# Entrance and gathers of a 32-expert mixture rebuilt: norm split without its shift, gathers of four experts, routing first, 16 weight buffers

## The chip, the core and the metric

The kernel runs on one core of a Trainium2 chip. The metric is device time in microseconds (us) from launch to end. Three runs of the kernel before took 2071.98 to 2072.4 us, median 2072.03.

## The reference, cut to what matters

256 tokens of width 1024, fp32, go through two hybrid blocks (state space and dilated attention, with gated feed-forward layers) and then through a second block: a convolution and gated-linear-attention mixer, a mixture of 32 experts, and a final modulated norm. The change touches the end of that mixer, the mixture and the final norm:

```python
h = h + ga1[:, None, :] * y                       # y = merged @ w_out (mixer)
u2 = modulate(rmsnorm(h, g_norm2[l]), sh2, sc2)   # norm * (1 + sc2) + sh2
y2 = hierarchical_moe(u2, ...)
h = h + ga2[:, None, :] * y2
return modulate(rmsnorm(h, g_final), shf, scf)

def hierarchical_moe(h, w_rg, b_rg, w_re, b_re, w1, w3, w2):
    lg = (t @ w_rg + b_rg); gsel = top_k(lg, 1)          # one of 4 groups
    le_sel = (t @ w_re + b_re) of that group             # its 8 experts
    top_v, top_i = lax.top_k(le_sel, 2)                  # two of them
    ...
    for e in range(32):
        hid = jax.nn.silu(t @ w1[e]) * (t @ w3[e])       # 1024 -> 512
        y = y + comb[:, e:e + 1] * (hid @ w2[e])         # 512 -> 1024
```

The weights of the 32 experts are 192 MB in fp32, and each of them has to come from HBM once.

## The kernel before, in words

The engines run from queues in program order; a scheduler of tiles puts in the semaphores. The words below go stage by stage through the end of the program.

**End of the mixer** (`mixer2`, lines 955 to 992). The product with `w_out` is made in two halves of 512 columns. After each half, VectorE makes the residual stream `x` of both 128-token tiles and `xg = x * G2`, where `G2` is the gain of the second norm times (1 + scale); TensorE transposes `xg` and multiplies it with the router's weights (L980); ScalarE takes the squares for the norm. `rsqrt` (L71 to L87) makes the reciprocal root in 12 small VectorE operations, after which L989 writes the 36 logits of each tile.

**Norm of the experts' input** (`norm2`, L1329). VectorE makes u = xg * rstd + sh2 for each tile (L1335), ScalarE its rounded part `u2h` (L1340), GpSimd the rest `u2l` (L1341). The pair hi + lo lets TensorE copy rows exactly.

**Routing** (`route`, L1197). Some 20 small VectorE operations find group, experts and weights; a prefix sum on TensorE (L1237, L1238) gives each token its slot in its expert, `pos` (L1240). An expert has 64 slots. A second part (L1244 on) makes the weights and counts.

**Gathers** (`gather`, L1412). For a batch of `BATCH = 8` experts VectorE compares the slot numbers with `pos` and so makes a one-hot matrix `sel` [256 tokens, 8 x 64] (L1417). For each of the 8 chunks kc of the model width, four matmuls (u2h and u2l, two token tiles) of 512 columns write the gathered inputs to a PSUM bank, and VectorE or ScalarE copy them to `T` (L1435, L1437). Batch 0 is gathered up front; each later batch is made beside the experts of the batch before it. `paced(..., 2, 1)` and `tick` drop one chunk (one piece) of a gather into TensorE's program at points between weight tiles. The pieces use the pool `tp` of two PSUM banks, which the transposes of the hidden layer and `slots` use too.

**Experts** (`experts`, L1530), in 16 pairs. A pair uses the two 64-column halves of the array, one expert each: `project` (L1469) for w1 and w3, `hidden` (transposes L1484, Silu L1488, product L1490), `down` (L1504) for the pair before, and `spread` (L1522), which adds the weighted rows into four accumulator banks. The weights come in pieces of 1 MB, 12 for a pair, on SyncE's DMA queue (L1392). There are RAWB + RAW2 + RAW3 + RAW4 = 4 + 3 + 2 + 3 = 12 buffers of 1 MB; a new load is issued when the matmuls of two buffers have been issued (`halves`, L1405).

**End** (`finish_rows` L1343, `finish` L1358). The rows of the last norm are loaded and made by GpSimd during the entrance. The tail multiplies the accumulators with ga2, adds the residual, takes the norm and writes out.

Of the kernel before, what the change touches and what calls it, by code (L numbers as in the profile page):

```python
# [9 lines left out]
F32 = mybir.dt.float32  # L10
# [38 lines left out]
class Kern:  # L49
# [21 lines left out]
    def rsqrt(self, src, n, scale, pool=None):  # L71

        nc, pool = self.nc, pool or self.small
        m = self.t(pool, [P, n], "nw_m")
        md = m.rearrange("p (a b) -> p a b", a=src.shape[1]) if len(src.shape) == 3 else m
        nc.vector.tensor_scalar(md, src, scale, EPS, op0=ALU.mult, op1=ALU.add)  # L76
        t = self.t(pool, [P, n], "nw_t")
        y = self.t(pool, [P, n], "nw_y", bufs=6)
        nc.vector.tensor_scalar(t.bitcast(I32), m.bitcast(I32), 1, None, op0=ALU.arith_shift_right)  # L79
        nc.vector.tensor_scalar(  # L80
            y.bitcast(I32), t.bitcast(I32), -1.0, float(0x5F3759DF), op0=ALU.mult, op1=ALU.add
        )
# [746 lines left out]
    def mixer2(self):  # L829
        nc, a, tc = self.nc, self.a, self.tc  # L830
        w_in = a["w_in_2"][0]
        with ExitStack() as outer:
# [124 lines left out]
            self.ss = self.t(self.small, [P, 2, 2], "ss", bufs=2)  # L957
            pl = [self.t(self.ax, [P, 512], "ax") for _ in range(2)]
            xTs = self.t(keep, [P, 2, D], "o")
            for nb in range(2):  # L960
                sl = slice(nb * 512, (nb + 1) * 512)
                ps = self.gemm_x(a["w_out_2"][0], nb * 512, 512, self.xh, self.xl)
                xT = xTs[:, nb, :].rearrange("p (c t) -> p c t", c=4)
                done = None
                for t in range(2):
                    with tc.issue_after(done) if done else ExitStack():
                        m = self.t(self.tmp, [P, 512], "xg")
                        nc.vector.tensor_mul(m, ps[t], ga1[:, sl])
# [4 lines left out]
                    for j in range(4):  # L973
                        nc.tensor.transpose(pt[:, j, :], xg[:, j * P : (j + 1) * P], self.ident)
                    nc.scalar.activation(xT[:, :, t * P : (t + 1) * P], pt, AF.Copy)
                    sq = self.t(self.tmp, [P, 512], "sq", bufs=1)
                    nc.scalar.activation(sq, self.x[:, t, sl], AF.Square, accum_out=self.ss[:, t, nb : nb + 1])
                    for j in range(4):
                        kc = nb * 4 + j
# [4 lines left out]
                if nb == 0:  # L984
                    self.moe_more()
            self.prep_end()
# [210 lines left out]
    def route(self, pool):  # L1197
# [36 lines left out]
        nc.vector.tensor_add(mb, o1, o2)  # L1234
# [3 lines left out]
        nc.tensor.matmul(pp[:, 32:64], self.ones, mb[:, 0, :], start=False, stop=True)  # L1238
        pos = self.t(pool, [P, 2, 32], "pos")
# [70 lines left out]
    def moe_final(self):  # L1310
        nc, a, tc = self.nc, self.a, self.tc
        with ExitStack() as ctx:
# [9 lines left out]
            route = self.route(lp)  # L1322
            self.norm2(lp, u2h, u2l)
            pos = next(route)
            rows = self.finish_rows(lp)
            comb, cnt = self.experts(lp, u2h, u2l, route, pos, acc)
            self.finish(lp, acc, rows, cnt, comb)

    def norm2(self, lp, u2h, u2l):  # L1329

        nc = self.nc
        w = self.t(lp, [P, 4, D], "T")
        for t in range(2):
            u = w[:, t, :]
# [8 lines left out]
    def finish_rows(self, lp):  # L1343

        nc, a = self.nc, self.a
        rows = [self.t(lp, [P, D], f"fin{j}") for j in range(3)]
        for dst, idx in zip(rows, (5, 7, 6)):
            nc.gpsimd.dma_start(dst, self.modd[0:1, idx * D : (idx + 1) * D].to_broadcast([P, D]))
        g = a["g_final_2"].rearrange("(o n) -> o n", o=1)
        for nb in range(2):  # L1350
            sl = slice(nb * 512, (nb + 1) * 512)
            gr = self.t(lp, [P, 512], "gu", bufs=4)
            nc.gpsimd.dma_start(gr, g[:, sl].to_broadcast([P, 512]))
            nc.gpsimd.tensor_scalar(rows[1][:, sl], rows[1][:, sl], 1.0, None, op0=ALU.add)
            nc.gpsimd.tensor_mul(rows[1][:, sl], rows[1][:, sl], gr)
        return rows

    def finish(self, pool, acc, rows, cnt, comb):  # L1358
        nc = self.nc
        ga2, Gf, shf = rows  # L1360
        yz = self.t(pool, [P, 4, D], "T")
        y, z = yz[:, 0:2, :], yz[:, 2:4, :]
# [49 lines left out]
    def gather(self, pool, b, u2h, u2l, pos, out, banks=None):  # L1412
# [12 lines left out]
        for kc in range(KD):  # L1425
            sl = slice(kc * P, (kc + 1) * P)
            pg = banks[kc % 4] if banks else self.t(self.tp, [P, 512], "tp")
            pg = pg.rearrange("p (e s) -> p e s", e=BATCH)
            for n, src in enumerate((u2h, u2l)):
                for t in range(2):  # L1430
                    nc.tensor.matmul(
                        pg, src[:, t, sl], sel[:, t], start=n == 0 and t == 0, stop=n == 1 and t == 1
                    )
# [96 lines left out]
    def experts(self, pool, u2h, u2l, route, pos, acc):  # L1530
# [6 lines left out]
        nxt = self.beside(self.gather(pool, 0, u2h, u2l, pos, batch, acc[0] + acc[1]))  # L1537
        sel0 = next(nxt[0])
        for e in range(0, NEXP, 2):
            b, ei = divmod(e, BATCH)  # L1540
            if ei == 0:
                self.drain(nxt)
                sel, T = batch
                if e == 0:
                    with self.tc.issue_after(sel0):
                        comb, combs, cnt = next(route)
# [4 lines left out]
            x = T[:, :, ei : ei + 2, :]  # L1551
            slots = self.beside(self.slots(pool, sel, ei, e, combs, so))
            gu = [self.project(pool, x, on_scalar)]
# [8 lines left out]
            last = h, so  # L1562
        self.drain()
        self.down(pool, NEXP - 2, last[0][0], *last[1], acc)
        self.drain()
        return comb, cnt

    def overflow(self, pool, cnt, comb, y, z, ga2):
# [3 lines left out]
        with tc.If(big > CAP):  # L1572
            w = self.t(self.s2, [P, 4, D], "T")
            G2, g, sh2, u = (w[:, j, :] for j in range(4))
            u2T = z.rearrange("p a b -> p (a b)").rearrange("p (k t) -> p k t", k=KD)
            nc.gpsimd.dma_start(G2, self.modd[0:1, 4 * D : 5 * D].to_broadcast([P, D]))
            nc.gpsimd.dma_start(g, a["g_norm2_2"].to_broadcast([P, D]))
            nc.gpsimd.dma_start(sh2, self.modd[0:1, 3 * D : 4 * D].to_broadcast([P, D]))
            nc.vector.scalar_tensor_tensor(G2, G2, 1.0, g, op0=ALU.add, op1=ALU.mult)
            for t in range(2):  # L1580
# [3 lines left out]
                nc.vector.tensor_add(u, u, sh2)  # L1584
                for k in range(KD):
                    pt = self.t(self.tp, [P, 512], "tp")
                    nc.tensor.transpose(pt[:, :P], u.rearrange("p (q k) -> p k q", k=KD)[:, k, :], self.ident)
                    nc.scalar.activation(u2T[:, k, t * P : (t + 1) * P], pt[:, :P], AF.Copy)
            nc.vector.memset(y, 0.0)
            with tc.For_i(0, NEXP, 1) as e:  # L1590
# [3 lines left out]
                hid = self.t(pool, [P, 4, 256], "gu_o")  # L1594
# [208 lines left out]
```

## Time and profile before

| | |
|---|---|
| median of 3 runs | 2072.03 us (2071.98 to 2072.4) |
| profiled execution, time | 2072.26 us |
| profiled execution, span from first to last instruction | 2070.4 us |
| mean granted TensorE clock (1 is 2.4 GHz) | 0.984 |
| TensorE busy | 1975.3 us, 95% of the span |
| VectorE, ScalarE, GpSimd busy | 60%, 43%, 10% |
| first matmul of an expert's weights begins | 1570.22 us |
| last matmul of the experts begins | 2052.42 us |

Rows of the trace give start and duration in us, engine (PE is TensorE, PEld its weight loads, DVE VectorE, ACT ScalarE, POOL GpSimd, SP SyncE), line, operation, output <- inputs, partitions x elements, and in brackets how long the engine stood idle before it, and what it waited for. A row with xN stands for N like instructions in a run. The end of a matmul is modelled, so starts are safer to subtract than durations. PEclk is the granted clock.

### The profile page before, as it was taken

The page shows a single profiled execution, that of the slowest core. Times are in us where ns is not written, and L with a number is a line of the kernel's source. Part 1 is how long each engine was busy: PE and PEld are TensorE (multiplying, and loading weights), DVE is VectorE, ACT ScalarE, POOL GpSimd, SP SyncE. Part 2 cuts the span into 40 slices and gives each one's busy share as a digit, 9 for nine tenths or more (in the row PEclk, how much of TensorE's full clock was granted, in tenths as well). Part 3 has the DMA queues.
Part 4 walks back from the last instruction along what each step waited for, and adds up shares of the span by engine and source line. Part 5 has one row for each costly group of instructions (what it writes and reads, how often), then busy time and mean ns, then how long its engine had stood idle before and what let it go on. Part 6 is the DMA issues. An engine that isn't in the chain of part 4 may idle for free. (4 is left out here: it accounts for less than half of the span.)

```text
span 2070.4 us, 25452 instructions
## 1 busy us (share of the span) xinstructions
PE 1975.3 (95%) x9734; PEld 1442.8 (70%) x9734; DVE 1232.4 (60%) x2027; ACT 899.3 (43%) x1371; POOL 217.3 (10%) x300
## 2 busy tenths in 40 slices
PE   8999999999999999999999999889978999999996
PEld 6888978788888888987788888877864433333332
DVE  5874897778766775797876556999762111110113
ACT  5444666645444444575745444766531111111111
POOL 1000222000000000023000000653011000000001
PEclk9999999999999999999999999999988999999998
DMA  8875543447776875542546556444766999999994
GB/s 276 283 276 189 163 138 102 160 162 259 262 251 225 269 253 178 181 162 82 166 135 201 182 171 205 124 132 153 266 224 253 421 418 375 421 367 421 420 420 177
DMA packets 193100, 493.11 MB, mean 238 GB/s; under 512 B 11832, under 2 KB 47600, under 8 KB 168400
## 3 DMA queue, kind: packets, MB, share of 16 engines
q1 hardware_dynamic: 185760, 479.32, 64.1%
q0 software_dynamic: 4992, 11.49, 1.9%
q8 instruction: 78, 1.28, 0.3%
q10 hardware_dynamic: 2224, 0.66, 0.2%
q14 instruction: 46, 0.38, 0.1%
HBM read 490.34 MB, written 1.08 MB: 237 GB/s over the span
## 5 line engine op out<-in xcount | busy, mean ns | idle before, releaser
L128 DVE TENSOR_TENSOR lo<-raw,hi 128x1024 fp32r<-128x1024 f32 (+1 forms) x462 | 572.8, 1240 | 290.1 <-ACT hi L127 289.7
L127 ACT ACTIVATE hi<-raw 128x1024 fp32r<-128x1024 f32 (+1 forms) x462 | 486.4, 1055 | 532.3 <-PE mm L174 462.5
L173 PE MATMUL mm<-lo,xh 128*128 128x512 f32 (+2 forms) x1200 | 460.4, 384 | 10.9 <-DVE lo L128 10.9
L172 PE MATMUL mm<-hi,xh 128*128 128x512 f32 (+2 forms) x1200 | 465.7, 389 | 0.4 <-ACT hi L127 0.4
L174 PE MATMUL mm<-hi,xl 128*128 128x512 f32 (+2 forms) x1200 | 459.3, 383 | 0.0
L173 PEld LDWEIGHTS mm<-lo,xh 128*128 128x128 f32 x1200 | 227.6, 190 | 59.4 <-DVE lo L128 15.1
L174 PEld LDWEIGHTS mm<-hi,xl 128*128 128x128 f32 x1200 | 227.4, 189 | 45.8
L172 PEld LDWEIGHTS mm<-hi,xh 128*128 128x128 f32 x1200 | 227.5, 190 | 45.6 <-ACT hi L127 0.8
L1469 PE MATMUL mm<-raw,T 128*64 128x512 f32 x1024 | 242.4, 596 | 0.0
L1469 PEld LDWEIGHTS mm<-raw,T 128*64 128x64 f32 x1024 | 72.9, 137 | 139.8 <-issue 137.1
L1504 PE MATMUL mm<-raw,H 128*64 128x512 f32 x512 | 148.6, 600 | 10.1 <-DVE gu L1474 10.1
L172 PE MATMUL mm<-hi,hh 128*128 128x512 f32 x352 | 139.1, 395 | 0.0
L174 PE MATMUL mm<-hi,hl 128*128 128x512 f32 x352 | 138.9, 394 | 0.0
L173 PE MATMUL mm<-lo,hh 128*128 128x512 f32 x352 | 138.5, 394 | 0.0
L1474 DVE COPY gu<-mm 128x512 f32<-128x512 f32 x16 | 11.1, 692 | 178.6 <-PE mm L1469 168.8
L1504 PEld LDWEIGHTS mm<-raw,H 128*64 128x64 f32 x512 | 45.9, 136 | 85.5 <-issue 62.5
L1512 ACT ACTIVATE yh<-mm,wsl 128x512 fp32r<-128x512 f32 x32 | 22.0, 688 | 181.7 <-PE mm L1504 181.7
L191 PE MATMUL mm<-xh,lo 128*128 128x256 f32 x320 | 91.2, 285 | 3.4 <-DVE lo L128 3.4
L189 PE MATMUL mm<-xh,hi 128*128 128x256 f32 x320 | 91.1, 287 | 0.8 <-ACT hi L127 0.8
L190 PE MATMUL mm<-xl,hi 128*128 128x256 f32 x320 | 91.2, 285 | 0.4 <-DVE xl L204 0.4
L759 DVE SCALAR_TENSOR_TENSOR macc<-raw,cact,macc 128x512 f32<-128x512 f32 x112 | 83.9, 749 | 2.4 <-DMA raw<-in_w_ada_dram 0.3
L1513 DVE SCALAR_TENSOR_TENSOR yl<-mm,wsl,yh 128x512 fp32r<-128x512 f32 x32 | 24.0, 750 | 94.3 <-ACT yh L1512 93.0
(428 smaller groups left out, 2739.1 us busy)
## 6 DMA issues: line engine op xcount, KB each, us to landing
raw<-in_w_dram SPq DMA_DIRECT2D x192, 1024.0 KB, 10.0
raw<-in_w_in_dram SPq DMA_DIRECT2D x71, 1024.0 KB, 5.2
raw<-in_ffn_w_up_dram SPq DMA_DIRECT2D x44, 1024.0 KB, 6.8
raw<-in_ffn_w_gate_dram SPq DMA_DIRECT2D x43, 1024.0 KB, 5.2
raw<-in_ffn_w_down_dram SPq DMA_DIRECT2D x40, 1024.0 KB, 5.1
raw<-in_w_ada_dram SPq DMA_DIRECT2D x24, 1024.0 KB, 5.3
raw<-in_w_out_dram SPq DMA_DIRECT2D x20, 1024.0 KB, 5.1
raw<-in_w_ada_f_dram SPq DMA_DIRECT2D x8, 1024.0 KB, 5.4
```

The lines of the kernel that those rows point to most:

```text
L127: nc.scalar.activation(h, r, AF.Copy)
L128: nc.vector.tensor_tensor(l, r, h.bitcast(F32), op=ALU.subtract)
L172: nc.tensor.matmul(ps[t][:, :w], xh[:, kc, sl], hi, start=kc == 0, stop=False)
L173: nc.tensor.matmul(ps[t][:, :w], xh[:, kc, sl], lo, start=False, stop=False)
L174: nc.tensor.matmul(ps[t][:, :w], xl[:, kc, sl], hi, start=False, stop=kc == kt - 1)
L189: nc.tensor.matmul(o, hi[:, sl], xh[:, kc, :], start=kc == 0, stop=False)
L190: nc.tensor.matmul(o, hi[:, sl], xl[:, kc, :], start=False, stop=False)
L191: nc.tensor.matmul(o, lo[:, sl], xh[:, kc, :], start=False, stop=kc == kt - 1)
L759: last = nc.vector.scalar_tensor_tensor(acc, raw[:, k, :], c, acc, op0=ALU.mult, op1=ALU.add)
L1469: nc.tensor.matmul(pg[s * CAP : (s + 1) * CAP, :], x[:, kc, s, :], w[:, k, :], start=kc == 0, stop=kc == KD - 1,)
L1504: nc.tensor.matmul(pd[nb][q, :], H[:, c, q], w[s][:, k, nb * 512 : (nb + 1) * 512], start=c == 0, stop=c == 3,)
L1513: nc.vector.scalar_tensor_tensor(yl, pd[nb], ws, yh.bitcast(F32), op0=ALU.mult, op1=ALU.subtract)
```

## The change

- The second half of the product with `w_out` is made in two parts of 256 columns, each with its own residual, transposes, router matmuls and squares. The three sums of squares are added by one reduction.
- `rsqrt` takes 10 operations in place of 12 (other constants, two steps in place of three).
- The split of the norm leaves out the shift: `u2h` is xg * rstd rounded by ScalarE (four instructions of 512 columns, strided), `u2l` the rest by VectorE (four, in `lows`). The shift `sh2`, now a column per chunk, is added where the gathered rows leave PSUM. GpSimd has no part in it.
- VectorE goes from the logits straight to routing; one `lows` operation stands ahead of `pos`, three behind `sel`. The second part of the routing comes after the first projection.
- A batch of the gather is four experts: 8 batches in place of 4, matmuls of 256 columns in place of 512. Batch 0 uses four accumulator banks at a time, u2h matmuls first.
- The rows of the last norm are loaded by SyncE behind the last expert weights, into weight buffers, and combined by one VectorE operation there.
- Weight buffers: 4 + 4 + 2 + 6 = 16 of 1 MB. `T` of half the size and the rows that are gone make room.

```diff
-RAW2 = 3
+RAW2 = 4
 RAW3 = 2
-RAW4 = 3
-BATCH = 8
+RAW4 = 6
+BATCH = 4
...
-            for nb in range(2):
-                sl = slice(nb * 512, (nb + 1) * 512)
-                ps = self.gemm_x(a["w_out_2"][0], nb * 512, 512, self.xh, self.xl)
+            for i, (c0, w) in enumerate(((0, 512), (512, 256), (768, 256))):
+                sl = slice(c0, c0 + w)
+                n = w // P
+                ps = self.gemm_x(a["w_out_2"][0], c0, w, self.xh, self.xl)
...
-            self.prep_end()
+            s2 = self.t(self.small, [P, 2], "ss2", bufs=2)
+            nc.vector.tensor_reduce(s2, ss, axis=AX.X, op=ALU.add)
+            self.rstd = self.rsqrt(s2, 2, 1.0 / D)
...
+        with self.tc.issue_after(done):
+            lows.pop(0)()
         pos = self.t(pool, [P, 2, 32], "pos")
...
-            nc.vector.scalar_tensor_tensor(
-                u.rearrange("p (k q) -> p q k", k=KD), self.xg[:, t, :].rearrange("p (q k) -> p q k", k=KD),
-                self.rstd[:, t : t + 1], self.sh2.rearrange("p (q k) -> p q k", k=KD),
-                op0=ALU.mult, op1=ALU.add,
-            )
-            nc.scalar.activation(u2h[:, t, :], u, AF.Copy)
-            nc.gpsimd.tensor_tensor(u2l[:, t, :], u, u2h[:, t, :].bitcast(F32), op=ALU.subtract)
...
+        def low(h, u, l, r):
+            return lambda: nc.vector.scalar_tensor_tensor(
+                l, u, r, h.bitcast(F32), op0=ALU.mult, op1=ALU.subtract
+            )
...
+                nc.scalar.activation(h, u, AF.Copy, scale=r)
+                lows.append(low(h, u, l, r))
...
-        yield i.ins
+        yield
+        with self.tc.issue_after(i.ins):
+            for low in lows:
+                low()
...
-            if kc % 2:
-                nc.vector.tensor_copy(T[:, kc], pg)
-            else:
-                nc.scalar.activation(T[:, kc], pg, AF.Copy)
+            for kc, pg in enumerate(pgs, k0):
+                sh = self.sh2[:, kc : kc + 1]
+                if kc % 2:
+                    nc.vector.tensor_scalar(T[:, kc], pg, sh, None, op0=ALU.add)
+                else:
+                    self.filled = nc.scalar.activation(T[:, kc], pg, AF.Identity, bias=sh).ins
...
-            nc.gpsimd.dma_start(dst, self.modd[0:1, idx * D : (idx + 1) * D].to_broadcast([P, D]))
...
+            nc.sync.dma_start(dst, self.modd[0:1, idx * D : (idx + 1) * D].to_broadcast([P, D]))
+        g = rows.pop()
+        nc.sync.dma_start(g, a["g_final_2"].rearrange("(o n) -> o n", o=1).to_broadcast([P, D]))
+        nc.vector.scalar_tensor_tensor(rows[1], rows[1], 1.0, g, op0=ALU.add, op1=ALU.mult)
         return rows
```

Two places of the program show how rows move. The first is TensorE in the third pair of a batch of eight, around the transposes of the hidden layer. `gu` are the projections, `raw` the weights, `mm` and `tp` PSUM banks, `csq` the identity. Before:

```order
L1469 MATMUL mm_14639<-raw_14511,T_13891 64x512
L1484 MATMUL tp_14666<-csq_66,gu_14637 128x128 x4
L1469 MATMUL mm_14639<-raw_14513,T_13891 64x512
...
L1504 MATMUL mm_14674<-raw_14558,H_14546 64x512
L1484 MATMUL tp_14707<-csq_66,gu_14664 128x128 x4
L1446 MATMUL tp_14730<-identr_320,sel_13876 128x128 x2
L1448 MATMUL tp_14730<-combs_13823,sel_13876 128x4 x2
L1504 MATMUL mm_14673<-raw_14560,H_14546 64x512
```

The same place of the same pair now (L1508 is L1484 of before, L1453 the gather, L1493 and L1528 the weights):

```order
L1493 MATMUL mm_14703<-raw_14528,T_14451 64x512
L1508 MATMUL tp_14750<-csq_66,gu_14701 128x128 x4
L1453 MATMUL tp_14771<-sel_14716,u2h_13737 128x256 x2
L1453 MATMUL tp_14771<-sel_14716,u2l_13738 128x256 x2
L1453 MATMUL tp_14789<-sel_14716,u2h_13737 128x256 x2
L1453 MATMUL tp_14789<-sel_14716,u2l_13738 128x256 x2
L1493 MATMUL mm_14703<-raw_14530,T_14451 64x512
...
L1508 MATMUL tp_14803<-csq_66,gu_14748 128x128 x4
L1453 MATMUL tp_14822<-sel_14716,u2h_13737 128x256 x2
L1453 MATMUL tp_14822<-sel_14716,u2l_13738 128x256 x2
L1453 MATMUL tp_14844<-sel_14716,u2h_13737 128x256
L1528 MATMUL mm_14757<-raw_14577,H_14620 64x512
```

A batch of eight spread its 8 pieces over two of its four pairs and left the other two free. Now each batch of four spreads 8 pieces of half the width over its two pairs, so that every pair but the last two has pieces between its weights.

The second place is VectorE from the logits (`lg`) to the first gather. Before (`T` is u, `rgm` to `rgf` and `gu` the routing, `cmisc` constants):

```order
L989 SCALAR_TENSOR_TENSOR lg_13660<-ax_13430,nw_y_13648,ch_13220 128x36
L1335 SCALAR_TENSOR_TENSOR T_13704<-T_13212,nw_y_13648 128x128x8 x2
L1211 TENSOR_REDUCE rgm_13712<-lg_13660 128x2
L1212 TENSOR_TENSOR gu_13711<-lg_13660,rgm_13712 128x8
...
L1234 TENSOR_TENSOR gu_13711<-gu_13711 128x64
L1240 TENSOR_TENSOR pos_13739<-mm_13736,gu_13711 128x64
L1417 TENSOR_TENSOR sel_13755<-cmisc_318,pos_13739 128x512 x2
```

Now:

```order
L998 SCALAR_TENSOR_TENSOR lg_13689<-ax_13395,nw_y_13679,ch_13185 128x36
L1220 TENSOR_REDUCE rgm_13744<-lg_13689 128x2
L1221 TENSOR_TENSOR gu_13743<-lg_13689,rgm_13744 128x8
...
L1243 TENSOR_TENSOR gu_13743<-gu_13743 128x64
L1345 SCALAR_TENSOR_TENSOR u2l_13738<-T_13174,nw_y_13679,u2h_13737 128x512
L1251 TENSOR_TENSOR pos_13772<-mm_13768,gu_13743 128x64
L1434 TENSOR_TENSOR sel_13774<-cmisc_316,pos_13772 128x256 x2
L1345 SCALAR_TENSOR_TENSOR u2l_13738<-T_13174,nw_y_13679,u2h_13737 128x512 x3
L1459 TENSOR_SCALAR T_13780<-acc_2698_13714,cact_13175 128x256
```

The two wide operations ahead of the routing are gone; in their place one operation of 512 stands where VectorE waits for the prefix sum, and three behind `sel`, of half the width.

## Rows read from the trace of the kernel before

**Rows 1.** Two stretches of 20 us: length, busy of each engine, PEclk, DMA share, GB/s.

```profile
1620.00:1640.00 20.00, 20.00 (x92) 8.09 (x89) 1.70 (x4) 1.58 (x3) 0.00 (x0) 1.00 1.01 421
1900.00:1920.00 20.00, 18.54 (x86) 6.95 (x86) 1.70 (x4) 1.58 (x3) 0.00 (x0) 1.00 1.01 422
```

**Rows 2.** Expert weight loads, L1392: who waited for it (us, times).

```profile
  PEld mm L1469: 0.9, 3
  PEld mm L1504: 0.7, 2
```

**Rows 3.** Timeline of VectorE in the entrance.

```profile
1539.63 0.69 DVE L971 TENSOR_TENSOR T<-x,sr 128x512 f32<-128x512 f32 x1
...
1543.92 0.26 DVE L989 SCALAR_TENSOR_TENSOR lg<-ax,nw_y,ch 128x36 f32<-128x36 f32 x1 [0.58 <-PE ax L980]
1544.10 3.78 DVE L1335 SCALAR_TENSOR_TENSOR T<-T,nw_y 128x1024 f32<-128x1024 f32 x2
...
1547.93 2.06 DVE L1212 TENSOR_TENSOR gu<-lg,rgm 128x8 f32<-128x8 f32 x1
1550.03 2.27 DVE L1214 SCALAR_TENSOR_TENSOR gu<-gu,cmisc 128x8 f32<-128x8 f32 x1
...
1556.97 0.22 DVE L1234 TENSOR_TENSOR gu<-gu 128x64 f32<-128x64 f32 x1
1558.35 0.23 DVE L1240 TENSOR_TENSOR pos<-mm,gu 128x64 f32<-128x64 f32 x1 [1.15 <-PE mm L1238]
1558.61 2.24 DVE L1417 TENSOR_TENSOR sel<-cmisc,pos 128x512 fp32r<-128x512 f32 x2
```

**Rows 4.** Timeline of TensorE from the first gather to the first weights.

```profile
1560.40 1.62 PE L1431 MATMUL acc<-sel,u2h 128*128 128x512 f32 x3 [1.60 <-DVE sel L1417]
...
1567.33 0.63 PE L1431 MATMUL acc<-sel,u2h 128*128 128x512 f32 x2
...
1569.20 0.63 PE L1431 MATMUL acc<-sel,u2h 128*128 128x512 f32 x2
...
1570.22 3.65 PE L1469 MATMUL mm<-raw,T 128*64 128x512 f32 x16
```

**Rows 5.** Two stretches of the first gather, columns as in rows 1.

```profile
1560.00:1564.00 4.00, 3.60 (x9) 2.85 (x10) 2.52 (x10) 1.25 (x4) 0.00 (x0) 0.50 0.00 0
1564.00:1566.00 2.00, 2.00 (x8) 1.58 (x7) 1.58 (x7) 0.33 (x1) 0.00 (x0) 0.69 0.02 4
```

**Rows 6.** Timeline of TensorE, one piece of the first hidden gather.

```profile
1593.12 3.65 PE L1469 MATMUL mm<-raw,T 128*64 128x512 f32 x16
1596.70 0.74 PE L1431 MATMUL tp<-sel,u2h 128*128 128x512 f32 x2
...
1597.83 3.65 PE L1469 MATMUL mm<-raw,T 128*64 128x512 f32 x16
```

**Rows 7.** Timeline of TensorE: two pairs with gathers, later one without.

```profile
1666.51 0.75 PE L1484 MATMUL tp<-csq,gu 128*128 128x128 f32 x4
...
1668.11 0.50 PE L1431 MATMUL tp<-sel,u2h 128*128 128x512 f32 x1 [0.51 <-DVE H L1490]
...
1735.25 0.75 PE L1484 MATMUL tp<-csq,gu 128*128 128x128 f32 x4
...
1918.41 0.75 PE L1484 MATMUL tp<-csq,gu 128*128 128x128 f32 x4
...
1929.70 7.09 PE L1469 MATMUL mm<-raw,T 128*64 128x512 f32 x32
...
1947.01 0.75 PE L1484 MATMUL tp<-csq,gu 128*128 128x128 f32 x4
```

**Rows 8.** Timeline of TensorE, matmuls of 258 columns in an earlier stage.

```profile
1299.75 0.28 PE L189 MATMUL mm<-oh,hi 128*128 128x258 f32 x1
...
1300.95 0.29 PE L190 MATMUL mm<-ol,hi 128*128 128x258 f32 x1
```

**Rows 9.** One group of VectorE: line, form xcount, busy us, mean ns, idle before.

```profile
L1011 DVE SCALAR_TENSOR_TENSOR sr<-sr 128x1024 f32<-128x1024 f32 x1 | 1.2, 1224 | 0.4 <-DMA sr<-in_g_norm_dram 0.4
```

More of the change, by code (lines that the diff above doesn't have):

```diff
@@ L27 @@
 NEXP = 32
+RC = 0.375**0.2
 CAP = 64
@@ L1194, in conv_norm, with route @@
         self.dump("zc", xc)
-    def route(self, pool):
+    def route(self, pool, lows):
         nc, lg = self.nc, self.lg
@@ L1233, in route @@
         mb = scratch(5)
-        nc.vector.tensor_add(mb, o1, o2)
+        done = nc.vector.tensor_add(mb, o1, o2).ins
         pp = self.t(self.mm, [P, 512], "mm")
@@ L1321, in moe_final, with norm2 @@
             u2l = self.t(lp, [P, 2, D], "u2l", F32R)
-            route = self.route(lp)
-            self.norm2(lp, u2h, u2l)
+            lows = self.norm2(u2h, u2l)
+            route = self.route(lp, lows)
             pos = next(route)
-            rows = self.finish_rows(lp)
-            comb, cnt = self.experts(lp, u2h, u2l, route, pos, acc)
+            comb, cnt, rows = self.experts(lp, u2h, u2l, lows, route, pos, acc)
             self.finish(lp, acc, rows, cnt, comb)
-    def norm2(self, lp, u2h, u2l):
+    def norm2(self, u2h, u2l):
@@ L1343, in finish_rows @@
-    def finish_rows(self, lp):
+        def low(h, u, l, r):
+            return lambda: nc.vector.scalar_tensor_tensor(
+                l, u, r, h.bitcast(F32), op0=ALU.mult, op1=ALU.subtract
+            )
+        lows = []
+        for k0 in range(0, KD, 4):
+            for t in range(2):
+                h, l = (
+                    x[:, t, k0 * P : (k0 + 4) * P].rearrange("p (k q) -> p k q", k=4) for x in (u2h, u2l)
+                )
+                u = self.xg[:, t, :].rearrange("p (q k) -> p k q", k=KD)[:, k0 : k0 + 4, :]
+                r = self.rstd[:, t : t + 1]
+                nc.scalar.activation(h, u, AF.Copy, scale=r)
+                lows.append(low(h, u, l, r))
@@ L1345, in finish_rows @@
+        return lows
+    def finish_rows(self):
         nc, a = self.nc, self.a
-        rows = [self.t(lp, [P, D], f"fin{j}") for j in range(3)]
+        rows = []
+        for _ in range(2):
+            w = self.eraw().rearrange("p a b -> p (a b)").rearrange("p (k n) -> p k n", n=D)
+            rows += [w[:, 0, :], w[:, 1, :]]
         for dst, idx in zip(rows, (5, 7, 6)):
-            nc.gpsimd.dma_start(dst, self.modd[0:1, idx * D : (idx + 1) * D].to_broadcast([P, D]))
-        g = a["g_final_2"].rearrange("(o n) -> o n", o=1)
@@ L1360, in finish @@
         ga2, Gf, shf = rows
-        yz = self.t(pool, [P, 4, D], "T")
-        y, z = yz[:, 0:2, :], yz[:, 2:4, :]
+        y = self.t(pool, [P, 2, D], "u2h")
+        z = self.t(pool, [P, 2, D], "u2l")
         parts = [(t, nb, slice(nb * 512, (nb + 1) * 512)) for t in range(2) for nb in range(2)]
@@ L1410, in halves, with gather @@
             self.tick()
-    def gather(self, pool, b, u2h, u2l, pos, out, banks=None):
+    def gather(self, pool, b, u2h, u2l, pos, out, banks=None, lows=()):
         nc = self.nc
@@ L1421, in gather @@
             )
-        yield i.ins
+        yield
+        with self.tc.issue_after(i.ins):
+            for low in lows:
+                low()
         T = self.t(self.s2 if b % 2 else pool, [P, KD, BATCH, CAP], "T")
         out += [sel, T]
[L1425 to L1428, printed above, removed]
+        n_k = len(banks) if banks else 1
+        for k0 in range(0, KD, n_k):
+            pgs = banks or [self.t(self.tp, [P, 512], "tp")]
+            pgs = [x[:, : BATCH * CAP].rearrange("p (e s) -> p e s", e=BATCH) for x in pgs]
             for n, src in enumerate((u2h, u2l)):
-                for t in range(2):
-                    nc.tensor.matmul(
-                        pg, src[:, t, sl], sel[:, t], start=n == 0 and t == 0, stop=n == 1 and t == 1
-                    )
-            if kc % 2:
-                nc.vector.tensor_copy(T[:, kc], pg)
-            else:
-                nc.scalar.activation(T[:, kc], pg, AF.Copy)
+                for kc, pg in enumerate(pgs, k0):
+                    sl = slice(kc * P, (kc + 1) * P)
+                    for t in range(2):
+                        nc.tensor.matmul(
+                            pg, src[:, t, sl], sel[:, t], start=n == 0 and t == 0, stop=n == 1 and t == 1
+                        )
+            for kc, pg in enumerate(pgs, k0):
+                sh = self.sh2[:, kc : kc + 1]
[3 more added lines that the diff above has]
+                    self.filled = nc.scalar.activation(T[:, kc], pg, AF.Identity, bias=sh).ins
             yield
@@ L1528, in down, with experts @@
         return self.beside(spread())
-    def experts(self, pool, u2h, u2l, route, pos, acc):
+    def experts(self, pool, u2h, u2l, lows, route, pos, acc):
         nc = self.nc
@@ L1536, in experts @@
         batch, last = [], None
-        nxt = self.beside(self.gather(pool, 0, u2h, u2l, pos, batch, acc[0] + acc[1]))
-        sel0 = next(nxt[0])
+        nxt = self.beside(self.gather(pool, 0, u2h, u2l, pos, batch, acc[0] + acc[1], lows))
         for e in range(0, NEXP, 2):
@@ L1543, in experts @@
                 sel, T = batch
-                if e == 0:
-                    with self.tc.issue_after(sel0):
-                        comb, combs, cnt = next(route)
+                filled = self.filled
                 batch = []
@@ L1551, in experts @@
             x = T[:, :, ei : ei + 2, :]
+            gu = [self.project(pool, x, on_scalar)]
+            if e == 0:
+                with self.tc.issue_after(filled):
+                    comb, combs, cnt = next(route)
             slots = self.beside(self.slots(pool, sel, ei, e, combs, so))
-            gu = [self.project(pool, x, on_scalar)]
             gu.append(self.project(pool, x, nc.vector.tensor_copy))
@@ L1562, in experts @@
             last = h, so
+        rows = self.finish_rows()
         self.drain()
@@ L1565, in experts @@
         self.drain()
-        return comb, cnt
+        return comb, cnt, rows
     def overflow(self, pool, cnt, comb, y, z, ga2):
@@ L1592, in rows @@
                     return a[nmk][0, ds(e, 1)].rearrange("o (p k) n -> p (o k) n", k=k)
-                hid = self.t(pool, [P, 4, 256], "gu_o")
+                hid = self.t(pool, [P, KD, 256], "T")
                 ws = {}
```

66 lines of the change are left out of this document (30 added, 36 removed).

## The prediction

> **What bounds the kernel now.** The sums are made against the profiled execution, 2072.26 us, of which 1.9 us lie around the span of 2070.4. It stands 0.23 us over the median of the runs, 2072.03; a time is given against that median by taking the 0.23 off. About 0.2% (4 us, so 2067.9 to 2076.2) is what a measurement of this kernel can tell from no change.
>
> I read the page first: TensorE is busy 95% of the span, and all that the change touches lies behind 1536 us. That stretch has two parts with different limits, and I take each by its own view.
>
> The *expert stage*, 1570.22 to about 2052, is read in stretches of 20 us. TensorE is busy 20.00 of 20 us in an early one and 18.54 in a later one, while the DMA engines are at share 1.01 and 421 GB/s in both [rows 1]. Two engines at their limit; the reader has to ask which waits for the other. The waits on the weight loads answer: project's weight loads on TensorE waited for a DMA 3 times, 0.9 us in all, in a stage of 482 us [rows 2]. So the transfers keep up, and TensorE's own program sets the pace. What is added to that program costs time, what is given to the DMA queue does not.
>
> The *entrance*, 1536 to 1570.22, is read on the timelines. Here VectorE is the chain: residual, norm, logits, then two wide operations of 3.78 us [rows 3], the routing, `pos`, `sel`. TensorE's first gather waits for `sel` [rows 4], and the first weight matmul at 1570.22 for the gather. What VectorE does in less time here moves the whole rest of the program forward.
>
> **The change part by part.**
>
> *Entrance up to the logits.* The six VectorE operations behind the last product are half as long: 0.69 each [rows 3], so 6 x 0.34 = 2.1 us less. Two steps of `rsqrt` go: by the small operations of this stretch, 0.22 each [rows 3], 0.4 us. Against it, the transposes and router matmuls of the third quarter now stand between the products on TensorE; I charge 1 us, an estimate between nothing and the 2.1 gained. Net -1.5 us.
>
> *Logits to routing.* The two operations of L1335 leave the path. They start at 1544.10 and take 3.78 [rows 3], less a little that overlaps: -3.5 us. Their successors are ScalarE's `u2h`, which runs beside the routing, and `u2l`, of which one of 512 columns stands in a place where VectorE waits 1.15 us for the prefix sum anyway [rows 3]. I cost it at nothing; without that cover it would be about half of one L1335, 0.9 us.
>
> *Routing.* L1212 and L1214 take 2.06 and 2.27 us for 8 columns, where an operation of 64 columns takes 0.22 [rows 3]. The long ones run while GpSimd makes `u2l`; GpSimd has none of that now. If they shrink to 0.22: -3.9 us. The clean operation of the same stretch speaks for it.
>
> *sel.* Two operations of 512 columns took 2.24 us [rows 3]; at 256, -1.1 us. The first gather starts 1.5 + 3.5 + 3.9 + 1.1 = 10.0 us earlier, at 1550.4.
>
> *First gather.* Before: 1560.40 to 1570.22, 9.8 us for 32 matmuls of 512 columns [rows 4]. It begins at the lower clock level (granted 0.50, 1.2 GHz) and is at the upper one from about 1565.2 on, since the stretch 1564 to 1566 has 0.69 [rows 5]; that is 4.8 us after it began, TensorE having had only the short prefix sums before. At the upper level eight matmuls of 512 columns take 1569.20 - 1567.33 = 1.87, 0.234 each [rows 4], and ten of 258 columns 1.20, 0.12 each [rows 8]. Now: 32 of 256 columns, for 4.8 us at twice 0.12, which is 20 of them, then 12 at 0.12: 6.2 us. -3.6 us. From both sides: at the upper level throughout 3.8 us (-6.0); at the lower throughout, with 1 us of waiting for the four banks, 8.7 us (-1.1).
>
> Entrance in all: **-13.6 us** (-11 to -16), first project at 1556.6.
>
> *Hidden gathers: before.* One piece in the early stage: 16 weight matmuls start at 1593.12, the next 16 at 1597.83 [rows 6], 4.71 us. Sixteen alone are 7.09 - 3.65 = 3.44 (32 against 16) [rows 6, 7]. So a piece costs 1.27, a batch of eight pieces 10.2 us. Of the 1.27, four matmuls at 0.234 are 0.94; 0.33 is for leaving the weights and coming back. Later, two pairs with a batch in them take 1735.25 - 1666.51 = 68.74 us, a pair without 1947.01 - 1918.41 = 28.60 [rows 7]; the batch costs 68.74 - 57.20 = 11.5. Three hidden batches, one early and two late: 10.2 + 2 x 11.5 = 33.3 us.
>
> A rule of the Trainium skill, "TensorEngine Tiling (Array Packing)", section Instruction Overhead, speaks of small pieces: a matmul has a fixed overhead of about 60 cycles, which shows only at a free size under that. By it halving the width halves the price, as 0.12 against 0.234 does for the matmuls; the 0.33 of a visit is not in it. By the rule alone seven batches of four would cost 3.5/3 of the three of eight, +5.6 us in place of what follows, and the sum would be 2064, rival B's time; its chance lies in B's.
>
> *Hidden gathers: now.* The number of visits doubles per expert: 7 batches of 8 pieces, 56 in place of 24. A piece of four matmuls of 256 costs 4 x 0.12 + 0.33 = 0.81, a batch 6.5 us where the stage is clean. Where it is not, a batch costs 11.5 less 32 x 0.114 = 3.6, so 7.9. There a second thing comes in: pieces share two PSUM banks with the transposes of the hidden layer, and already a gather waits 0.51 us for the product H to free one [rows 7]. A piece of 0.48 in place of 0.94 covers 0.45 less of such a wait; at three places in a batch (Silu, H, one copy out) that is 0 to 1.4 us. The copies out of PSUM get shorter too, so I take the middle, 0.7: 8.6 us. The stage is clean in the early pairs, where TensorE has no idle time [rows 1], which is about two batches: 2 x 6.5 + 5 x 8.6 = 56 us. **+22.7 us**. From both sides: all seven at 6.5, +12.2; five at 7.9 + 2.8 (the waits twice as long), +33.2.
>
> *Four more buffers.* They let loads run 10 us further ahead, of which TensorE can get back its 1 us of waits [rows 2]. I take 0.
>
> *Tail.* The rows of the last norm come behind the last weights and need one VectorE operation of 1024 columns, 1.22 us [rows 9]. VectorE has time for it beside the last `down`; if it comes late, +1.2. `rsqrt` gives 0.4. I take 0 (-0.4 to +0.8).
>
> Sum: -13.6 + 22.7 + 0 = +9.1, 2081.4 by the profiled execution, **2081 us** against the median.
>
> **The rivals.**
>
> *A, the transfers carry the stage.* If the stage ran at the rate of the weights, the added pieces would be hidden. For it: share 1.01 [rows 1], and the 16 buffers start it fuller. Against it: waits of 1 us [rows 2], and a pair with pieces is 28.6 + 4.3 = 32.9 us, where 12 MB at 421 GB/s take 29.9. Then only the entrance counts: 2072.0 - 13.6 = 2058. It decides if project waits for its DMA more than 10 us in all. The Trainium skill's "SBUF — State Buffer", in its section on the bandwidth pool, says that HBM is almost always the end-to-end bottleneck; here it is near it, and by the waits not it. 6%.
>
> *B, the pieces fall into idle time (faster).* In the later stretches TensorE stands 1.46 of 20 us idle [rows 1], 2.1 us in a pair. Before, six pairs had pieces, now 14; if the eight new ones fill that time, 8 x 2.1 = 16.7 us come back: +22.7 - 16.7 = +6.0, and 2072.0 - 13.6 + 6.0 = 2064. Against it: the pieces stand behind the transposes, not ahead of them, and the pairs with pieces [rows 7] were no cheaper than the clean price. It decides if the idle share falls below 0.7 in 20. 8%.
>
> *C, every batch at the clean price.* No waits for banks, 6.5 for each: 2072.0 - 13.6 + 12.2 = 2071, no change that can be told. The late batches of before, 11.5 against 10.2, speak against it. 17%.
>
> *D, dearer.* The waits for banks twice as long and the first gather at the lower clock: -11.1 + 33.2, 2094. 12%.
>
> **How the numbers follow.** The forecast, a sum between 2074 and 2089, has 57%, D 12%, C 17%, B 8%, A 6%. Faster by over 0.2%: A and B, 14%. Within: C and the low end of the forecast, 20%. Slower: 66%. The range 2064 to 2092 leaves out A and most of D. The forecast's own range is 2074 to 2089.
>
> **What would show it.** Right: first project near 1556.6, L1335's like and 2-us routing operations gone; then pairs of 32 to 33 us in which gather runs of half the length stand twice as often; project's waits for its DMA still a few us. The gain of the entrance would be seen whole at 1557 and given back at about 2 us a pair. Wrong: a batch of four that costs under 7 us late in the stage (C, B), or pairs of 30 us with weight loads waiting for DMA (A).

## The result: 11 us slower, and the profile after

The changed kernel takes 2083.09 us (median of 5 runs, 2081.77 to 2083.91) against 2071.98 before; the ratio is 1.0053, 95% interval 1.0038 to 1.0068. The profiled execution took 2083.79 us with a span of 2081.9 us, 11.5 longer than before. It splits in four places, each measured from row to row:

| stretch | before | after | difference | forecast |
|---|---|---|---|---|
| start to VectorE's first multiplication of the last mixer's merge (L951, now L957) | 1495.99 | 1493.64 | -2.4 | none |
| from there to the first project | 74.23 | 61.21 | -13.0 | -13.6 |
| from there to the last row of the experts' matmuls (its start) | 482.2 | 508.1 | +25.9 | +22.7 |
| from there to the end of the span | 18.0 | 19.0 | +1.0 | 0 |

The first line is not sharp: between profiled executions of kernels whose program ahead of the entrance is that of the changed one, the mark lies between 1491.51 (E11) and 1494.16 (E9). "Project" is the first matmul of an expert's weights.

**Entrance.** VectorE's timeline of the changed kernel, from the logits to `sel`:

```profile
1541.78 0.42 DVE L998 SCALAR_TENSOR_TENSOR lg<-ax,nw_y,ch 128x36 f32<-128x36 f32 x2
1542.23 0.16 DVE L1220 TENSOR_REDUCE rgm<-lg 128x2 f32<-128x8 f32 x1
1542.43 0.17 DVE L1221 TENSOR_TENSOR gu<-lg,rgm 128x8 f32<-128x8 f32 x1
...
1542.63 0.17 DVE L1223 SCALAR_TENSOR_TENSOR gu<-gu,cmisc 128x8 f32<-128x8 f32 x1
...
1546.45 1.16 DVE L1345 SCALAR_TENSOR_TENSOR u2l<-T,nw_y,u2h 128x512 fp32r<-128x512 f32 x1
1547.68 0.22 DVE L1251 TENSOR_TENSOR pos<-mm,gu 128x64 f32<-128x64 f32 x1
1547.94 0.76 DVE L1434 TENSOR_TENSOR sel<-cmisc,pos 128x256 fp32r<-128x256 f32 x2
1548.62 3.34 DVE L1345 SCALAR_TENSOR_TENSOR u2l<-T,nw_y,u2h 128x512 fp32r<-128x512 f32 x3
```

It answers to [rows 3]. The logits are followed at once by the routing, and the operations that took 2.06 and 2.27 us take 0.17. The `u2l` piece ahead of `pos` takes 1.16 us and ends before the prefix sum's result is used. TensorE's timeline, and two stretches (columns as in rows 1), answer to [rows 4, 5]:

```profile
1548.51 2.05 PE L1453 MATMUL acc<-sel,u2h 128*128 128x256 f32 x8 [0.87 <-DVE sel L1434]
...
1554.85 1.51 PE L1493 MATMUL mm<-raw,T 128*64 128x512 f32 x6
```

```profile
1548.00:1552.00 4.00, 3.49 (x16) 3.52 (x17) 4.00 (x6) 0.60 (x2) 0.00 (x0) 0.50 1.01 428
1552.00:1556.00 4.00, 4.00 (x24) 3.08 (x24) 2.35 (x6) 2.06 (x4) 0.00 (x0) 0.79 0.44 182
```

The first gather begins 11.9 us earlier than before and takes 6.34 us in place of 9.82. It still begins at the lower clock level; the mean of 0.79 in the last stretch puts the rise at about 1553.7.

**Expert stage.** The two stretches of [rows 1] are as busy as before, 20.00 and 18.54 us of 20, and the DMA share of the later one has fallen from 1.01 to 0.95. No weight load of TensorE waited for a DMA any more; so the reader sees that the stage grew by TensorE's own work:

```profile
1620.00:1640.00 20.00, 20.00 (x93) 8.10 (x90) 3.07 (x5) 2.86 (x6) 0.00 (x0) 1.00 1.02 422
1900.00:1920.00 20.00, 18.54 (x82) 6.58 (x82) 1.76 (x5) 1.58 (x3) 0.00 (x0) 1.00 0.95 380
```

The timeline of TensorE answers to [rows 7]; five of its rows are the second hidden transposes of a pair, from which pairs are measured there too; one is a wait for a PSUM bank, and one a run of four weight matmuls between two pieces:

```profile
1686.24 0.75 PE L1508 MATMUL tp<-csq,gu 128*128 128x128 f32 x4
...
1687.84 0.38 PE L1453 MATMUL tp<-sel,u2h 128*128 128x256 f32 x1 [0.38 <-DVE H L1514]
...
1693.29 1.93 PE L1528 MATMUL mm<-raw,H 128*64 128x512 f32 x4
...
1720.66 0.75 PE L1508 MATMUL tp<-csq,gu 128*128 128x128 f32 x4
...
1752.59 0.75 PE L1508 MATMUL tp<-csq,gu 128*128 128x128 f32 x4
...
2014.71 0.75 PE L1508 MATMUL tp<-csq,gu 128*128 128x128 f32 x4
...
2043.33 0.75 PE L1508 MATMUL tp<-csq,gu 128*128 128x128 f32 x4
```

A pair with pieces takes 34.42 us (1686.24 to 1720.66) or 31.93, one without 28.62 (2014.71 to 2043.33). Two pairs with one batch of four cost 66.35 - 57.24 = 9.1 us over two free ones; a batch of eight had cost 11.5. There are five such late batches where there had been two, 5 x 9.1 - 2 x 11.5 = 22.5 of the 25.9 us.

The run of four shows a cost that neither the matmuls of a piece nor the bank waits hold. Weight matmuls mostly start two by two, one in each half of the array: sixteen take 3.44 us [rows 6, 7]. These four start one by one, 0.43 us apart, and so take as long as eight. Counted over the stage in the traces, 136 of the 1536 weight matmuls start alone before and 164 now; 28 x 0.215 = 6.0 us of the 25.9, by an estimate from the 3.44. Why a cut leaves some of them alone the traces do not show.

**Tail.** VectorE's timeline:

```profile
2065.49 0.69 DVE L1387 TENSOR_TENSOR x<-x,u2h 128x512 f32<-128x512 f32 x1
2066.10 1.22 DVE L1372 SCALAR_TENSOR_TENSOR raw<-raw,raw 128x1024 f32<-128x1024 f32 x1
2067.23 4.04 DVE L1387 TENSOR_TENSOR x<-x,u2h 128x512 f32<-128x512 f32 x3
...
2072.45 1.20 DVE L79 TENSOR_SCALAR nw_m<-ss 128x2 f32<-128x2 f32 x1
```

The operation for the last norm's row (L1372) stands between two residual additions, in the tail itself, and takes its 1.2 us there.

### The profile page after: what moved, and what is told of

Read it like the earlier page. It is cut to its first block, busy times and chain, and to the rows that moved or that the text cites. A ratio compares the mean times of both kernels' runs of the same rounds, so it can differ in the third digit from the quotient of the medians.

```text
span 2081.9 us, 25805 instructions
## 1 busy us (share of the span) xinstructions
PE 1990.5 (96%) x9910; PEld 1453.8 (70%) x9910; DVE 1229.4 (59%) x2018; ACT 908.3 (44%) x1395; POOL 204.2 (10%) x289
## 5 line engine op out<-in xcount | busy, mean ns | idle before, releaser
L179 PE MATMUL mm<-lo,xh 128*128 128x512 f32 (+1 forms) x1216 | 463.3, 381 | 11.4 <-DVE lo L134 11.4
L178 PE MATMUL mm<-hi,xh 128*128 128x512 f32 (+1 forms) x1216 | 468.1, 386 | 0.2 <-ACT hi L133 0.2
L180 PE MATMUL mm<-hi,xl 128*128 128x512 f32 (+1 forms) x1216 | 461.5, 380 | 0.0
L1493 PE MATMUL mm<-raw,T 128*64 128x512 f32 x1024 | 246.2, 597 | 0.0
L1493 PEld LDWEIGHTS mm<-raw,T 128*64 128x64 f32 x1024 | 73.2, 137 | 137.7 <-issue 134.1
L1528 PE MATMUL mm<-raw,H 128*64 128x512 f32 x512 | 154.1, 602 | 10.1 <-DVE gu L1498 10.1
L1528 PEld LDWEIGHTS mm<-raw,H 128*64 128x64 f32 x512 | 45.2, 136 | 83.7 <-issue 58.5
L1459 DVE TENSOR_SCALAR T<-tp,cact 128x256 f32<-128x256 f32 x28 | 13.5, 483 | 144.1 <-PE tp L1453 144.1
L1461 ACT ACTIVATE T<-tp,cact 128x256 f32<-128x256 f32 x28 | 13.3, 474 | 182.8 <-PE tp L1453 182.8
```

Of the source, the lines that this page charges most:

```text
L178: nc.tensor.matmul(ps[t][:, :w], xh[:, kc, sl], hi, start=kc == 0, stop=False)
L179: nc.tensor.matmul(ps[t][:, :w], xh[:, kc, sl], lo, start=False, stop=False)
L180: nc.tensor.matmul(ps[t][:, :w], xl[:, kc, sl], hi, start=False, stop=kc == kt - 1)
L1493: nc.tensor.matmul(pg[s * CAP : (s + 1) * CAP, :], x[:, kc, s, :], w[:, k, :], start=kc == 0, stop=kc == KD - 1,)
L1528: nc.tensor.matmul(pd[nb][q, :], H[:, c, q], w[s][:, k, nb * 512 : (nb + 1) * 512], start=c == 0, stop=c == 3,)
```

## The experiments

The median of the kernel before was 2071.4 to 2073.7 us beside these runs. "Stage" is the time from the first project to the last row of the experts' matmuls, "batch" the price of a late hidden batch, as worked out above, in the profiled execution.

**E1, pieces of two chunks.**

```diff
-            pgs = banks or [self.t(self.tp, [P, 512], "tp")]
+                pg2 = self.t(self.tp, [P, 512], "tp")
+                pgs = [pg2[:, j * w : (j + 1) * w] for j in range(2)]   # w = 256, n_k = 2
```

> The changed kernel with pieces of two chunks: eight gather matmuls of 256 columns fill one PSUM bank, 28 visits of TensorE to the hidden gathers in place of 56, same matmuls, same copies out. Theory (a hidden gather is paid by the visit and by waits for the two shared banks): a late batch of four falls from 9.1 us to about 5.5, seven batches by 24 us, 2059 us (2052 to 2066). Rival (paid by the instruction, a matmul of 256 costs nearly what one of 512 does): nothing changes, 2078 or more.

Measured: 2062.62 us (4 runs), ratio 0.995, 0.9933 to 0.9967. Stage 488.6, batch 5.9:

```profile
1651.38 0.75 PE L1516 MATMUL tp<-csq,gu 128*128 128x128 f32 x4
...
1684.22 0.75 PE L1516 MATMUL tp<-csq,gu 128*128 128x128 f32 x4
...
1714.50 0.75 PE L1516 MATMUL tp<-csq,gu 128*128 128x128 f32 x4
```

32.84 + 30.28 - 57.2 = 5.9. The same 224 hidden matmuls of 256 columns in half as many pieces cost 19.4 us less, so the price does not go by the instruction. A piece is not yet a visit, since some stand together or beside the transposes: counted in the traces, the stream of weight matmuls is broken by others 73 times before, 88 times in the changed kernel and 80 times in E1. Waits for the two banks fell too (late in the stage from 5.0 to 2.5 us), and 116 weight matmuls start alone in place of 164.

**E2, batches of eight with the rest of the change; E3, batches of four in the kernel before.**

```diff
-RAW2 = 4
+RAW2 = 3
-RAW4 = 6
-BATCH = 4
+RAW4 = 5
+BATCH = 8
```

> The changed kernel with batches of eight again, 14 weight buffers so that it fits; everything else of the change stays. Theory (the batch size gives the stage its 25.9 us and the rest of the change is gain): first project 3.6 us later than in the changed kernel, at 1558.5; stage back to 482 us; tail 1 us longer; 2061 us. Rival (the stage is longer by other parts: the shift in the copies out, the buffers): 2075 or more.

> The kernel before with batches of four and nothing else. Theory: hidden gathers +25.9 us, first gather 3.6 less, 2094 us (2090 to 2098). Rival (batches of four are cheap, the other parts of the change cost the time): 2080 or less.

E2: 2060.13 us, ratio 0.9938 (0.9922 to 0.9955); first project at 1557.3, stage 482.1, which is that of before to 0.1 us. So the longer stage comes with the batch size, and the rest of the change adds nothing to it net. The parts do not agree as closely: a late batch of E2 costs 12.3 us (11.5 before), and with 14 buffers its weight loads waited 3.3 us for DMA. E3: 2102.43 us, ratio 1.0141 (1.0124 to 1.0158): the sign and the cause as expected, the size 8 us too small. Its batch costs 10.3 us (two pairs from 1668.29 to 1735.80), 1.2 more than in the changed kernel; five of them make about 6 of the 7.4 us by which its stage, 515.5, is longer. TensorE's waits for a PSUM bank of the shared pool, 1660 to 2060, in E3 and in the changed kernel (us in all, times, longest):

```profile
PE tp L1431 <- DVE T L1435: 2.6, 5, 0.5
PE tp L1431 <- DVE H L1490: 2.5, 5, 0.5
PE tp L1431 <- ACT T L1437: 2.4, 5, 0.5
PE tp L1446 <- DVE H L1490: 1.9, 5, 0.4
PE tp L1431 <- ACT H L1488: 1.1, 5, 0.2
```

```profile
PE tp L1453 <- DVE H L1514: 3.9, 9, 0.5
PE tp L1453 <- ACT H L1512: 1.1, 5, 0.2
```

10.5 against 5.0 us in about five batches, 1.1 us a batch, which is about the difference. The pieces and the slots stand in another order in E3; that the order makes the waits was not tested by itself.

**E4, 12 buffers in the changed kernel** (RAW2 = 3, RAW4 = 3).

> The changed kernel with 12 weight buffers as before (4 + 3 + 2 + 3). Theory (TensorE sets the pace, buffers bring nothing): 2083 us, within 2. Rival (the fuller start carries part of the stage): 2088 or more.

2083.97 us (2082.8 to 2084.59), which cannot be told from the 2083.09 with 16. In the profiled execution the weight loads do wait for DMA again (who waited for L1409: us, times), and the stage is 1.7 us longer, 509.8:

```profile
  PEld mm L1493: 2.4, 8
```

By these numbers the four buffers bring 2 us at most.

**E5, GpSimd beside the routing.** The kernel, with 15 buffers, computes two subtractions that nothing reads.

```diff
+            nc.gpsimd.tensor_scalar(junk[:, 0:2], self.rstd, 1.0, None, op0=ALU.mult)
+            for t in range(2):
+                nc.gpsimd.tensor_tensor(junk, self.xg[:, t, :], self.xg[:, t, :], op=ALU.subtract)
```

> The changed kernel (14 or 15 buffers, which e4 showed to cost nothing) with two useless GpSimd subtractions of 1024 columns beside the routing, the kind of work that u2l was. Theory (GpSimd beside lengthens VectorE's small operations): some of the routing operations that now take 0.17 us take 2 us or so again, the first project starts 3 to 5 us later than the 1554.85 of the changed kernel. Rival (the long ones came from something else, such as the wide operations ahead of them): all stay at 0.17 to 0.23 us, first project within 0.5 us.

GpSimd's and VectorE's timelines:

```profile
1540.92 3.87 POOL L1337 TENSOR_TENSOR junk<-T 128x1024 f32<-128x1024 f32 x2
```

```profile
1540.96 0.16 DVE L1220 TENSOR_REDUCE rgm<-lg 128x2 f32<-128x8 f32 x1
1541.15 1.68 DVE L1221 TENSOR_TENSOR gu<-lg,rgm 128x8 f32<-128x8 f32 x1
...
1543.07 0.16 DVE L1225 TENSOR_REDUCE rgf<-gu 128x2 f32<-128x8 f32 x1
1543.27 1.55 DVE L1226 TENSOR_TENSOR gu<-cmisc,rgf 128x8 f32<-128x8 f32 x1
```

Two routing operations went from 0.17 to 1.68 and 1.55 us; the way from the merge to the first project is 63.7 us in place of 61.2, 2.5 longer, in one run and less than the 3 to 5 expected. GpSimd's two subtractions end at 1542.81 and 1544.79, the two long operations at 1542.83 and 1544.82: VectorE waits for the end of a GpSimd operation, and the reduction ahead of it, which reads one tensor, stays at 0.16. That is what the Trainium skill says in "SBUF — State Buffer", section Who interferes with whom: a VectorE operation with two SBUF inputs and a GpSimd one that reads SBUF block one another for a whole instruction. The trace agrees.

One tensor alone is no safeguard, though. In the tail of the changed kernel, the first operation of `rsqrt` (L79, one input of 2 columns) takes 1.20 us, 2072.45 to 2073.64, and ends with the last of GpSimd's operations there, at 2073.62; in the entrance, with GpSimd idle, it takes 0.17. GpSimd's row:

```profile
2067.49 6.12 POOL L1389 TENSOR_TENSOR u2h<-x,raw 128x512 f32<-128x512 f32 x4 [590.33 <-DVE raw L1372]
```

**E6 and E9, pieces beside the hidden transposes**: another list of points at which pieces are given out, for batches of four (E6, on E1) and of eight (E9, on E2).

```diff
-                    nxt = self.beside(paced(self.gather(...), 2, 1))
+                    nxt = self.beside(at(self.gather(...), (1, 2, 4, 8, 10) if b else (1, 2, 4, 6, 8)))
```

> As e1 (pieces of two chunks, batches of four), with the pieces given out at other points, so that in TensorE's program each one stands beside the hidden transposes, where TensorE leaves the weights anyway: no visits of its own. Theory (price by the visit): a late batch of four falls from 5.9 us to the matmuls alone, 32 x 0.117 = 3.7, plus 0.3; 2062.6 - 7 x 1.9 = 2049 us (2045 to 2055). Rival (waits for the two shared banks take the place of the visits): 2059 or more.

> As e2 (batches of eight, rest of the change kept), with the pieces given out beside the hidden transposes of all four pairs. Theory: a late batch of eight falls from 12.3 us to the matmuls alone, 32 x 0.234 = 7.5, plus 0.6; three batches by 12 us; 2048 us (2044 to 2054). Rival (pieces beside the transposes wait for the banks): 2057 or more.

Both missed: 2062.84 us (2060.5 to 2065.2) and 2061.41 us, no better than E1 and E2. Every pair of E6 takes 31.20, a batch 5.2 rather than 4.0, though no bank wait is left. TensorE's timeline of E6, from one second transposes to the next and behind them:

```profile
1682.16 0.75 PE L1528 MATMUL tp<-csq,gu 128*128 128x128 f32 x4
...
1713.37 0.75 PE L1528 MATMUL tp<-csq,gu 128*128 128x128 f32 x4
1713.87 0.48 PE L1473 MATMUL tp<-sel,u2h 128*128 128x256 f32 x2
...
1714.89 0.33 PE L1490 MATMUL tp<-identr,sel 128*128 128x128 f32 x1
1715.15 3.65 PE L1548 MATMUL mm<-raw,H 128*64 128x512 f32 x12
1718.73 0.33 PE L1490 MATMUL tp<-identr,sel 128*128 128x128 f32 x1
1718.89 0.33 PE L1492 MATMUL tp<-combs,sel 128*128 128x4 f32 x2
```

The piece stands right, but the two matmuls that turn `sel` for the slots, which had followed the transposes as two, are now apart, with 12 weight matmuls between: a new visit in place of the old one. In the ten late pairs the stream of weight matmuls is broken 49 times, as in E1; of what the late batches gained, 2.5 us are the bank waits that E1 had and E6 has not. In E9 a pair takes 31.27, a batch 10.7 in place of 12.3. In both, the late batches fell by more than the stage (3.6 against 1.3 us in E6, 3.3 against 0.8 in E9), so the first pairs, where the pieces have other points, cost some 2 us more; why is not shown.

**E10, both pieces of a pair together behind the first transposes** (points 2, 4, 4, 10, 10).

> As e1 (pieces of two chunks, batches of four), with both pieces of a pair given out so that they stand together behind the first hidden transposes. E6 put one behind each of the two transposes; there the second piece pushed the slot matmuls into a visit of their own, 0.7 us a pair. Theory (price by the visit and by what a piece displaces): a late pair takes 28.6 + 16 x 0.117 + 0.2 of a bank wait = 30.7, a batch 4.1 us, stage 481, 2055 us (2052 to 2059). Rival (two pieces at once wait for the two banks and the gain is lost): 2060 or more.

2055.47 us (2054.64 to 2058.34, 5 runs), ratio 0.9922, 0.9908 to 0.9935: 16 us faster than the kernel before and 27 faster than the changed one, with its entrance, its buffers and its batches of four. TensorE:

```profile
1683.69 0.75 PE L1528 MATMUL tp<-csq,gu 128*128 128x128 f32 x4
...
1702.74 0.75 PE L1528 MATMUL tp<-csq,gu 128*128 128x128 f32 x4 [0.68 <-ACT gu L1578]
1703.25 0.48 PE L1473 MATMUL tp<-sel,u2h 128*128 128x256 f32 x2
...
1714.19 0.75 PE L1528 MATMUL tp<-csq,gu 128*128 128x128 f32 x4
```

Pairs of 30.50; a batch costs 61.0 - 57.2 = 3.8 us, which is 32 x 0.117 = 3.7, the matmuls alone. Stage 480.9. The stream of weight matmuls is broken 72 times in place of 88, 124 of them start alone in place of 164, and the gather matmuls wait for no bank late in the stage; what each of the three is worth was not tested by itself.

**E11, the product in two parts again.**

> The changed kernel with the second half of the w_out product in one part again. Theory (the split is worth what the forecast charged, 2.1 of shorter operations less 1 of matmuls in between): from the last product matmul to the logits 1 to 2 us longer than in the changed kernel, first project 1 us or so later against the product's end less what the product ends earlier. Rival (the split brings nothing net): the logits come within 0.3 us as long after the start of the second half.

2080.98 us in one run. From the first residual operation of the first half (L975) to the second logits (L998), VectorE of E11 and of the changed kernel:

```profile
1517.79 0.68 DVE L975 TENSOR_TENSOR xg<-mm,gain 128x512 f32<-128x512 f32 x1
...
1531.63 0.69 DVE L975 TENSOR_TENSOR xg<-mm,gain 128x512 f32<-128x512 f32 x1 [7.51 <-PE mm L180]
...
1539.64 0.26 DVE L998 SCALAR_TENSOR_TENSOR lg<-ax,nw_y,ch 128x36 f32<-128x36 f32 x1 [1.19 <-PE ax L987]
```

```profile
1519.91 0.68 DVE L975 TENSOR_TENSOR xg<-mm,gain 128x512 f32<-128x512 f32 x1
...
1536.75 0.42 DVE L975 TENSOR_TENSOR xg<-mm,gain 128x256 f32<-128x256 f32 x1 [5.02 <-PE mm L180]
...
1541.78 0.42 DVE L998 SCALAR_TENSOR_TENSOR lg<-ax,nw_y,ch 128x36 f32<-128x36 f32 x2
```

22.1 us without the split (1539.90 - 1517.79) and 22.3 with it (1542.20 - 1519.91); before, it was 21.9. The rival holds: the split brings nothing. Behind the last product the way to the logits is 2.8 us shorter (1542.20 - 1536.75 = 5.45 for 1539.90 - 1531.63 = 8.27), and the last product comes 3.0 us later (16.84 for 13.84 after the first row).

**E12 and E13, the reciprocal root alone**: that of before in the changed kernel, and that of the changed kernel in the kernel before.

> The changed kernel with the reciprocal root of 12 operations again, in all of its 21 uses. Theory (the shorter root took about 3 us out of the stages ahead of the entrance, most of it in the first mixer between 295 and 365 us, and 0.4 us each in entrance and tail): product of the mixer's end at 1496 in place of 1493.6, 2083.1 + 3.5 = 2086.6 us (2085 to 2088). Rival (the 2.4 us ahead of the entrance are scatter between executions): 2083.9 or less.

> The kernel before with the reciprocal root of 10 operations in its 21 uses, and nothing else. Theory: the same 3.5 us the other way, 2068.5 us (2067 to 2070), the product of the mixer's end at 1492 to 1494 in place of 1496. Rival (scatter): within 1 us of the kernel before.

E12 2087.35 us (2086.24 to 2089.14), 4.3 more than the changed kernel, or 3.8 when each is taken against the kernel before of its own measurement; E13 2067.73 us against 2072.43, ratio 0.9979, 0.997 to 0.9988. The first multiplication of the last mixer's merge stands at 1497.51 in E12 and 1491.64 in E13, against 1493.64 and 1495.99. The shorter root is worth about 4 us, most of it ahead of the entrance, 0.4 in the tail, and nothing in the entrance: from the merge to the first project it is 74.19 us in E13 and 74.23 before, 61.27 in E12 and 61.21 in the changed kernel.

## Why the prediction was right, point by point

The forecast was +9.1 us, the profiled executions differ by 11.5, and the cause is the one that was named: the entrance gains, and more pieces in TensorE's program take back more. Some of the agreement is luck, since a term that was missing (-2.4) covers most of one that was too small (+25.9 for +22.7).

**TensorE sets the pace of the stage** (rival A wrong). E4 and the waits show it: with 16 buffers no weight load waited for DMA, and with 12 they waited 2.4 us in a stage of 510.

**Routing and norm** were right. The forecast had -8.5 us from the logits to the first gather; it was 16.2 to 6.3, -9.9, since other routing operations had been held up too. E5 shows GpSimd as the cause. The first gather gave 3.5 for 3.6.

**Up to the logits** it was wrong: -1.5 forecast, +0.4 found (22.3 us for 21.9). The step that failed is the 1 us charged for what now stands between the products: the last product comes 3.0 us later, and the split is worth nothing (E11). The 0.4 us for `rsqrt` failed too. Before, the second logits wait 0.58 us for TensorE's router matmuls [rows 3], so VectorE was not the last to be ready, and the shorter root alone brought nothing here (E13).

**Ahead of the entrance** a term was missing. `rsqrt` was counted in two places, and it has 21 uses; E12 and E13 measure about 4 us for all of them. That it made up for what the next point lacked is luck.

**Hidden gathers** had the right mechanism and a size 3.2 us too small. The late batch was 9.1 for 8.6, 2.7 us over five; the early batches differ by the rest. The term that was too small is the rise over 7.9, taken as 0.7 and measured as 1.2. It was put down to longer bank waits, and these rose by 0.5 us a batch, from 0.5 (1.0 us in two late batches) to 1.0 (5.0 in five). The other 0.7 had no term: the forecast kept 0.33 us a visit, where the cut stream also leaves weight matmuls that start alone. E1 and E10 bound the price: 3.7 us are matmuls, and all else is 5.4 in the changed kernel, 2.2 in E1, 0.1 in E10. Rival B was wrong as a forecast of this change: from 1660 to 2040 TensorE was idle for 19.3 us before and 22.3 now. C was wrong too: no late batch was cheaper than 9.1. D was wrong in both of its conditions: the waits rose by 0.5 us a batch where it had 2.8, and the first gather reached the upper clock level.

**Tail**: +1.0 for 0, outside the -0.4 to +0.8 that was allowed. I thought VectorE would make the row beside the last `down`; in VectorE's program it stands behind the first residual addition.

## What to carry to other kernels

Where a small job is fed into a stream that keeps an engine busy, count the places where it enters, not only its instructions: here 56 pieces of half the size cost 26 us more than 24, and the same matmuls cost only their own time once they stood where the engine left the stream anyway. After moving pieces, look at what they push aside (E6), since that can take back the gain. And when a helper is changed, count all its callers.

## What the runs showed of the hardware that was not expected

A GpSimd operation on SBUF holds up a VectorE operation of 8 columns with two inputs in SBUF until it ends: 1.68 us for 0.17 (E5). The same shows for one of 2 columns with a single input, 1.20 us for 0.17, in the tail. Where weight matmuls of 64 columns start alone, 0.43 us pass for each; where they start two by two, 0.215. And a matmul of 256 columns next to others costs 0.117 us on TensorE, with nothing for leaving the 64-column weights beside transposes (E10), whereas a visit of its own cost about 0.33 us besides [rows 6].
